# Both sample groups of an attention head turned, summed and closed together, the second cached values in the places of the cached keys, and fourteen heads' outputs kept whole

## The chip, the core and the metric

The kernel runs on one core of a Trainium2 chip. The metric is the device time of one execution in microseconds (us): the median of three runs before the change is 2847.96 us (2842.49 to 2850.93). The engines are TensorE (PE: matmuls and transposes; PEld is its weight load), VectorE (DVE), ScalarE (ACT), GpSimd (POOL) and SyncE (SP), which here only issues transfers.

## The reference

One step of a streaming encoder with two layers: a recurrent one (RG-LRU), then one of stick-breaking attention with 16 heads of 128. There is one prompt of 512 frames and there are 8 samples of 16 new frames each, and each sample has 512 cached keys and values. Only attention is touched here:

```python
def sb_block(q, q_pos, k, v):
    z = jnp.einsum('bqhd,bshd->bhqs', q, k).astype(jnp.float32) * (HEAD_DIM ** -0.5)
    mask = jnp.arange(k.shape[1])[None, :] < q_pos[:, None]
    log_keep = jnp.where(mask, jax.nn.log_sigmoid(-z), 0.0)
    log_after = lax.cumsum(log_keep, axis=3, reverse=True) - log_keep
    attn = jnp.where(mask, jnp.exp(jax.nn.log_sigmoid(z) + log_after), 0.0)
    return jnp.einsum('bhqs,bshd->bqhd', attn, v.astype(jnp.float32)).astype(q.dtype)

def stick_breaking_mixer(hn, k_all, v_all, w_in, w_out):
    q, zg = jnp.split(hn @ w_in, 2, axis=-1)
    o = stick_breaking(q.reshape(B, T, N_HEADS, HEAD_DIM), k_all, v_all)
    return (o.reshape(B, T, D_ATT) * jax.nn.silu(zg)) @ w_out
```

## The kernel before, in words

All is computed for 640 columns: 512 of the prompt, 128 of the samples. Products of large matrices are done in three matmuls of split numbers (`mm3`, lines 112 to 114: high times high, high times low, low times high), each split being a copy on ScalarE and a subtraction on VectorE. The recurrent layer, its output and the shared keys and values fill the span up to about 1985 us; then come the attention heads and the output product.

`heads` (line 1885) goes through 16 heads. While head h does its attention, the query and gate of head h+1 are computed in nine steps `q` of the generator `query`; in the last head the steps go to the output product instead. They are most of TensorE's work. The order of the steps inside a head is written out by hand in the strings `ORDER` and `LAST`; a scheduler then places the instructions on each engine's queue in about that order, moving what is ready by its own costs, and each queue is executed in order. The steps:

- `P`: the prompt's scores (tiles z, lines 1715 to 1717) and their weights (`sticks`, line 1641: on ScalarE Abs, Exp, Ln and a last Exp in line 1662; on VectorE an add, a scan and a subtraction; on GpSimd the mask). `X`: the samples' scores against their new keys (zn).
- `S0`, `S1`: scores of four samples each against their cached keys (zc, line 1757), weights into es0 and es1. The keys lie in two tiles ck of 128x1024 fp32. `S0` asks for the second group's keys; the step `N` (`cached_keys`, line 1692) for the next head's first.
- `V0`, `V1`: the prompt's weights turned on TensorE (pa, line 1727) and split into ath and atl (lines 1738, 1739).
- `T0`, `T1`: a sample group's weights turned (pas, line 1781) and copied by ScalarE to at. `T0` asks for the first group's cached values (cv).
- `O`: the prompt's output (po, lines 112 to 114), then the loads of the second group's cached values into the places of atl and ath (cva, cvb, line 1773), and of its new values on GpSimd's queue (line 1767).
- `M0`, `M1`: a sample group's output: 16 small matmuls against cached values (pos, line 1790) and 4 against new ones (line 1793), copied to ob. `C0`, `C1`: that output turned back (pot, line 1799), times the gate (line 1804).
- `L`, `K`: the next head's keys loaded (kr) and split (kh, kl, lines 1326, 1328). `U`, `W`: its values, loaded into the rest of cvb's place, and split. The gate's silu is made inside the query steps (ez, lines 1468 to 1473).

At the end of `C1` of heads 3, 5, 7, 9, 11 and 13 (`WHOLE`) the output is stored as it is, in fp32, and split when the output product loads it (`load` in `out_product`, lines 968, 969). Heads 0, 1, 2, 4, 6, 8, 10 and 12 split it at once (lines 1818, 1819) and store both halves (line 1821). Head 14 stays split in SBUF, head 15 whole.

PSUM has eight banks: two named halves, a ring of two (`one`) and a ring of four (`quad`).

Of the kernel before, what the change touches and what calls it, by code (L numbers as in the profile page):

```python
# [12 lines left out]
F32 = mybir.dt.float32  # L13
# [38 lines left out]
class Trunk:  # L52
# [1280 lines left out]
    def query_sums(self, ap):  # L1333
# [3 lines left out]
        flat = lambda tag: ap.tile([P, 3, 512], F32R, tag=tag, name="sum", bufs=1).rearrange("p a n -> p (a n)").bitcast(F32)  # L1337
# [179 lines left out]
    def query(self, h, ap):  # L1517
# [36 lines left out]
        def rest(a, c, u2, p5):  # L1554

            w = wl.pop(0), wl.pop(0)
            plain(c, w, 0)
            evac(halves[0], c, u2, ALU.add)
            self.scaled_query(0, halves[0], qh, ql, qs)
            yield  # L1560
            plain(a, w, 1)
            evac(halves[1], a, p5, ALU.add)
            self.scaled_query(1, halves[1], qh, ql, qs)
            with self.tc.issue_after(self.scaled):
                fill("wl", 3)
                fill("wh", 3)
            if h < NHEAD - 1:
                self.silu(ap, z, 0)
            yield
# [131 lines left out]
    def attention(self, h, ap, qkv, zs):  # L1701
# [17 lines left out]
        ath = ap.tile([P, 3, 512], F32R, tag="ath", name="ath", bufs=1)  # L1719
        atl = ap.tile([P, 3, 512], F32R, tag="atl", name="atl", bufs=1)  # L1720

        def spread(e, *rows, new=False):
# [5 lines left out]
            put = new_turn(0, ps) if new else lambda: None  # L1728
            parts, c = [], 0
            for i in rows:  # L1730
                m, q = min(i + 1, 3), slice(P * i, P * i + P)
                parts.append((ps[:, c : c + P * m].rearrange(pd, d=P), ath[:, :m, q], atl[:, :m, q]))
                if i == 3:
                    parts.append((ps[:, 384:], ath[:, 1, 0:P], atl[:, 1, 0:P]))
                c += P * (i + 1)
# [6 lines left out]
        def new_turn(g, ps):  # L1742

            tr(ps[0:TS, 384:], st[f"es{g}"][:, PAST : PAST + TS], self.ident)
            an = st["an"] = ap.tile([TS, P], F32, tag="an", name="an", bufs=1)

            def put():
                with self.tc.high_priority(200):
                    V.tensor_copy(an, ps[0:TS, 384:])

            return put

        def sample_scores(g):
# [10 lines left out]
        def new_values(g, t):  # L1764
            dma = (nc.gpsimd if g else nc.sync).dma_start
            rows = O["v"][TP + 64 * g : TP + 64 * g + 64, P * h : P * h + P]
            dma(t, rows.rearrange("(b t) d -> t b d", t=TS))
            return t
# [7 lines left out]
        def sample_turn(g):  # L1776
            e = st[f"es{g}"]
            st["cv"] = st["early"] if g else [cached_values(2 * u) for u in range(2)]
            ps = one("pas")
            for i in range(4):  # L1780
                tr(ps[:, P * i : P * i + P], e[:, P * i : P * i + P], self.ident)
            at = st["at"] = ap.tile([P, 4, P], F32, tag="at", name="at", bufs=1)
            A.activation(at, ps.rearrange(pd, d=P), AF.Copy)

        def sample_out(g):
            at, cvs = st["at"], st["cv"]
            po, an = one("pos"), st["an"]
            for i in range(4):
                for j in range(4):
                    mm(po[32 * j : 32 * j + 32, 0:P], at[:, i, 32 * j : 32 * j + 32], cvs[j // 2][:, 4 * (j % 2) + i, :],  # L1790
                       start=i == 0, stop=False, **kw)
            for j in range(4):
                mm(po[32 * j : 32 * j + 32, 0:P], an[:, 32 * j : 32 * j + 32], st["vn"][g][:, j, :], start=False, stop=True, **kw)
            ob = st["ob"] = ap.tile([P, P], F32, tag="ob", name="ob", bufs=1)
            A.activation(ob, po[:, 0:P], AF.Copy)

        def sample_close(g):
            ps = one("pot")
            tr(ps[:, 0:P], st["ob"], self.ident)
            if g == 0:  # L1800
                new_turn(1, ps)()
            cs = slice(TP + 64 * g, TP + 64 * g + 64)
            tv = "p (j t) -> p j t"
            V.tensor_tensor(o[:, cs].rearrange(tv, t=TS), ps[:, 0:P].rearrange(tv, t=32)[:, :, 0:TS],
                            zs[:, cs].rearrange(tv, t=TS), ALU.mult)
            if g == 1 and h == NHEAD - 1:
                self.local[h] = o
            elif g == 1 and h in self.STAY:
# [5 lines left out]
            elif g == 1 and h in self.WHOLE:  # L1814
                nc.gpsimd.dma_start(self.od[0][P * h : P * h + P, :], o)
            elif g == 1:
# [36 lines left out]
        def prompt_out():  # L1853
            po = zt("po")
            for i in range(3, -1, -1):
                th, tl = (x[:, 1, 0:P] if i == 3 else x[:, i, P * i :] for x in (ath, atl))
# [12 lines left out]
        st = {"vn": [new_values(0, ap.tile([TS, 4, P], F32, tag="vn", name="vn", bufs=1))], "early": []}  # L1869
        steps = {"P": prompt_scores, "X": new_scores, "O": prompt_out}  # L1870
        for g in range(2):
            steps[f"V{g}"] = lambda g=g: prompt_turn(g)
            steps[f"T{g}"] = lambda g=g: sample_turn(g)
            steps[f"M{g}"] = lambda g=g: sample_out(g)
            steps[f"C{g}"] = lambda g=g: sample_close(g)
# [5 lines left out]
    WHOLE = (3, 5, 7, 9, 11, 13)  # L1881
    LAST = "P c1 X S0 q q q S1 V0 q q T0 V1 Z O M0 T1 q q C0 M1 q C1 q"
    ORDER = "P q q c1 X S0 q q S1 V0 q q T0 V1 L q O U M0 T1 N K q C0 M1 W q"

    def heads(self, count=NHEAD):
        with self.pool("att") as ap:
# [11 lines left out]
            before, self.spare = {}, None  # L1898
            for h in range(count):
# [6 lines left out]
                for step in (self.ORDER if more else self.LAST).split():  # L1906
# [7 lines left out]
                    elif step == "c1":  # L1914
# [150 lines left out]
```

## Time and profile before

| | |
|---|---|
| profiled execution | 2848.22 us, span 2846.5 us, mean granted clock 0.998 |
| three runs | 2842.49, 2847.96, 2850.93 us |
| end of the first query | about 1984 to 2012 us |
| head 0 | about 2012 to 2060 us |
| heads 1 to 14 | about 2060 to 2605 us |
| head 15, with the first steps of the output product | 2605 to 2641 us |
| the rest of the output product | 2641 to 2833 us |
| rows of y, stores | 2833 to 2846.5 us |

The profile is of one execution, with times from the start of its span. A group or a wait is named by line, engine and tiles (out<-in). "A <- B" in a list of waits means that A's engine was idle until B was done. A stretch's row has the busy time and the number of instructions of each engine, the granted clock of TensorE (1.00 is full), the DMA engines' busy share and GB/s. Rows of a timeline give start, length, engine, line and, at the end in brackets, the idle time before it with what ended it. Matmuls overlap, so that their start, not their length, tells how fast they follow each other.

### The profile page before, as it was taken

The page shows a single profiled execution, that of the slowest core. Times are in us where ns is not written, and L with a number is a line of the kernel's source. Part 1 is how long each engine was busy: PE and PEld are TensorE (multiplying, and loading weights), DVE is VectorE, ACT ScalarE, POOL GpSimd, SP SyncE. Part 2 cuts the span into 40 slices and gives each one's busy share as a digit, 9 for nine tenths or more (in the row PEclk, how much of TensorE's full clock was granted, in tenths as well). Part 3 has the DMA queues.
Part 4 walks back from the last instruction along what each step waited for, and adds up shares of the span by engine and source line. Part 5 has one row for each costly group of instructions (what it writes and reads, how often), then busy time and mean ns, then how long its engine had stood idle before and what let it go on. Part 6 is the DMA issues. An engine that isn't in the chain of part 4 may idle for free.

```text
span 2846.5 us, 48073 instructions
## 1 busy us (share of the span) xinstructions
PE 2778.0 (98%) x18340; PEld 2454.0 (86%) x18340; DVE 2032.9 (71%) x3344; ACT 1667.3 (59%) x2862; POOL 426.9 (15%) x726
## 2 busy tenths in 40 slices
PE   6999999999999999999999999999999999999998
PEld 4799999999999987777777899967888888887887
DVE  7678777777677766766966866667877777777335
ACT  5466556655566655665756555553666766666223
POOL 0022212222222211111120000122101011011000
PEclk9999999999999999999999999999999999999999
DMA  9966767667666665685686333585476565668636
GB/s 338 328 147 155 164 160 161 148 164 164 158 149 163 149 228 202 203 251 181 222 286 216 100 107 114 173 274 202 131 215 193 187 198 168 205 197 267 189 111 229
DMA packets 245447, 540.57 MB, mean 190 GB/s; under 512 B 23048, under 2 KB 106120, under 8 KB 244064
## 3 DMA queue, kind: packets, MB, share of 16 engines
q1 hardware_dynamic: 198448, 375.08, 41.0%
q0 software_dynamic: 46768, 162.41, 23.0%
q8 instruction: 144, 2.36, 0.3%
q14 instruction: 87, 0.71, 0.1%
HBM read 498.01 MB, written 39.40 MB: 189 GB/s over the span
## 4 chain that ended last, share of the span: by engine, by line
PE 81%; DMA 4%; DVE 3%; ACT 2%; issue 2%; POOL 0%; SPq 0%; DVEq 0%; POOLq 0%; ACTq 0%
PE acc L112 7%; PE acc L114 6%; PE acc L113 6%; PE pa L112 4%; PE pa L114 4%; PE pa L113 4%; PE psh L112 4%; PE psh L114 4%; PE psh L113 4%; PE pc L114 3%; PE pc L112 3%; PE pc L113 3%; PE acck L112 2%; DMA cvb<-cache_v_dram 2%; PE acck L113 2%; PE acck L114 2%
## 5 line engine op out<-in xcount | busy, mean ns | idle before, releaser
L112 PE MATMUL acc<-wh,yh 128*128 128x512 f32 x940 | 369.6, 394 | 0.4 <-ACT wh L97 0.3
L113 PE MATMUL acc<-wl,yh 128*128 128x512 f32 x940 | 366.9, 390 | 1.5 <-DVE wl L98 1.4
L114 PE MATMUL acc<-wh,yl 128*128 128x512 f32 x940 | 365.6, 390 | 2.0 <-DVE yl L969 2.0
L98 DVE TENSOR_TENSOR wl<-wr,wh 128x1024 fp32r<-128x1024 f32 x151 | 186.2, 1237 | 215.7 <-ACT wh L97 215.2
L97 ACT ACTIVATE wh<-wr 128x1024 fp32r<-128x1024 f32 x151 | 159.6, 1058 | 266.8 <-PE acc L114 219.5
L112 PEld LDWEIGHTS acc<-wh,yh 128*128 128x128 f32 x940 | 176.2, 188 | 53.6 <-issue 16.1
L114 PEld LDWEIGHTS acc<-wh,yl 128*128 128x128 f32 x940 | 176.3, 188 | 39.8 <-DVE yl L969 2.8
L113 PEld LDWEIGHTS acc<-wl,yh 128*128 128x128 f32 x940 | 176.5, 188 | 39.3 <-DVE wl L98 4.1
L202 DVE TENSOR_TENSOR wa<-wa 128x1024 bf16<-128x1024 f32 (+1 forms) x160 | 191.3, 1247 | 10.0 <-ACT wa L201 9.6
L114 PE MATMUL pa<-xs,wl 128*128 128x320 f32 x630 | 194.8, 309 | 0.5 <-DVE wl L98 0.5
L112 PE MATMUL pa<-xs,wh 128*128 128x320 f32 x630 | 194.7, 309 | 0.0
L113 PE MATMUL pa<-xs,wh 128*128 128x320 f32 x630 | 194.7, 309 | 0.0
L97 ACT ACTIVATE wh<-sum 128x896 fp32r<-128x896 f32 x102 | 96.9, 950 | 143.2 <-PE pa L113 46.8
L201 ACT ACTIVATE wa<-wa 128x1024 bf16<-128x1024 f32 x160 | 159.8, 1047 | 25.0 <-DVE wa L202 12.1
L553 POOL DMA_DIRECT2D sum<-w_in_a_dram x90 | 79.4, 886 | 491.8 <-DVE wl L98 209.8
L112 PE MATMUL psh<-nh,wl 128*128 128x320 f32 x480 | 150.8, 314 | 0.0
L114 PE MATMUL psh<-nh,wl 128*128 128x320 f32 x480 | 148.4, 309 | 0.0
L113 PE MATMUL psh<-nl,wl 128*128 128x320 f32 x480 | 148.2, 309 | 0.0
L97 ACT ACTIVATE wh<-rv 128x256 fp32r<-128x256 f32 (+1 forms) x108 | 51.8, 480 | 145.6 <-PE pa L113 95.2
L114 PE MATMUL pc<-xs,wl 128*128 128x320 f32 x420 | 129.8, 309 | 0.7 <-DVE wl L98 0.7
L112 PE MATMUL pc<-xs,wh 128*128 128x320 f32 x420 | 130.1, 310 | 0.0
L113 PE MATMUL pc<-xs,wh 128*128 128x320 f32 x420 | 129.7, 309 | 0.0
(504 smaller groups left out, 8606.6 us busy)
## 6 DMA issues: line engine op xcount, KB each, us to landing
wa<-w_ada_dram POOLq DMA_DIRECT2D x120, 512.0 KB, 5.1
wr<-w_out_a_dram SPq DMA_DIRECT2D x96, 512.0 KB, 4.5
sum<-w_in_a_dram POOLq DMA_DIRECT2D x90, 448.0 KB, 5.7
wa<-w_ada_dram SPq DMA_DIRECT2D x72, 512.0 KB, 6.6
wr<-w_in_b_dram SPq DMA_DIRECT2D x64, 512.0 KB, 5.4
ck<-cache_k_dram SPq DMA_DIRECT2D x64, 512.0 KB, 5.9
wr<-w_out_b_dram SPq DMA_DIRECT2D x55, 512.0 KB, 4.0
raw<-w_in_a_dram SPq DMA_DIRECT2D x60, 448.0 KB, 4.0
```

Source lines behind the costliest of these rows:

```text
L97: self.split_at = nc.scalar.activation(hi[:, :n], raw, AF.Copy).ins
L98: nc.vector.tensor_tensor(lo[:, :n], raw, hi[:, :n].bitcast(F32), ALU.subtract)
L112: mm(out, sh, mh, start=start, stop=False, **kw)
L113: mm(out, sh, ml, start=False, stop=False, **kw)
L114: return mm(out, sl, mh, start=False, stop=stop, **kw)
L201: nc.scalar.activation(parts[i], raw, AF.Copy)
L202: nc.vector.tensor_tensor(parts[2] if i else raw, raw, parts[i], ALU.subtract)
L553: self.nc.gpsimd.dma_start(self.big[tag], self.quarter(w, i), accum_op=ALU.add)
```

## The change

Both sample groups are turned in one step `T` (the second group's transposes in a bank of the other ring), and the turned weights are copied back over es0 and es1 instead of into at. One step `M` sums both: first group's cached values, both groups' new values, second group's cached values. One step `C` in the next head closes both with two transposes and one product on VectorE. The second cached values are asked for in `S1`, into the two places of ck which its scores have just read. New values of all eight samples come in one load on the SP queue, at the head's start.

The next head's values are loaded into ath's place as a whole tile. ath and atl are laid out as rows of 1280 instead of 3x512, with the fourth block at 896. The first silu half waits for the last exponential of the sample weights on ScalarE (`issue_after`). All of heads 0 to 13 are `WHOLE`: one store, and the split in the output product. Before the first head, its keys and first cached keys are asked for ahead of the first query, and the keys no longer wait for the query's last load.

```diff
@@ flat tiles of query_sums, query
-        flat = lambda tag: ap.tile([P, 3, 512], F32R, tag=tag, name="sum", bufs=1).rearrange("p a n -> p (a n)").bitcast(F32)
+        flat = lambda tag: ap.tile([P, 2 * T], F32R, tag=tag, name="sum", bufs=1).bitcast(F32)
...
             if h < NHEAD - 1:
-                self.silu(ap, z, 0)
+                with self.tc.issue_after(self.weighed):
+                    self.silu(ap, z, 0)
@@ keys_load, values_load
-        with self.tc.issue_after(self.last_load):
+        with self.tc.issue_after(self.last_load) if h else ExitStack():
...
-        tile, self.spare = self.spare, None
-        if tile is None:
-            tile = ap.tile([P, 3, 512], F32R, tag="ath", name="vr", bufs=1).bitcast(F32)
-        raw = tile[:, 0, :].rearrange("p (t d) -> p t d", d=P)
+        tile = ap.tile([P, 2 * T], F32R, tag="ath", name="vr", bufs=1).bitcast(F32)
+        raw = tile[:, :TP].rearrange("p (t d) -> p t d", d=P)
@@ new_turn: both groups in V1
+            for g in range(2):
+                tr(ps[0:TS, 256 + P * g : 384 + P * g], st[f"es{g}"][:, PAST : PAST + TS], self.ident)
+            an = st["an"] = ap.tile([TS, 2 * P], F32, tag="an", name="an", bufs=1)
@@ sample_scores
             if g == 0:
                 self.ck = self.cached_keys(h, 1, ap)
+            else:
+                places = [ap.tile([P, 2, PAST], F32, tag="ck", name="cva", bufs=2) for _ in range(2)]
+                st["early"] = [cached_values(NB // 2 + 2 * u, c.rearrange("p a (i d) -> p (a i) d", d=P)) for u, c in enumerate(places)]
@@ sample_turn, sample_out, sample_close
+        def sample_turn():
+            st["cv"] = [cached_values(2 * u) for u in range(2)] + st["early"]
+            for g, ring in enumerate((one, zt)):
+                e, ps = st[f"es{g}"], ring("pas")
+                for i in range(4):
+                    tr(ps[:, P * i : P * i + P], e[:, P * i : P * i + P], self.ident)
+                A.activation(e[:, :PAST], ps, AF.Copy)
...
+            cached(0)
+            for g in range(2):
                 for j in range(4):
+                    mm(po[32 * j : 32 * j + 32, P * g : P * g + P], an[:, P * g + 32 * j : P * g + 32 * j + 32], st["vn"][:, 4 * g + j, :],
+                       start=False, stop=g == 0, **kw)
+            cached(1)
+            ob = st["ob"] = ap.tile([P, 2 * P], F32, tag="ob", name="ob", bufs=1)
+            A.activation(ob, po[:, : 2 * P], AF.Copy)
...
+            for g in range(2):
+                tr(ps[:, P * g : P * g + P], st["ob"][:, P * g : P * g + P], self.ident)
+            V.tensor_tensor(o[:, TP:].rearrange(tv, t=TS), ps[:, : 2 * P].rearrange(tv, t=32)[:, :, 0:TS],
+                            zs[:, TP:].rearrange(tv, t=TS), ALU.mult)
@@ prompt_out
             V.tensor_tensor(o[:, :TP], po, zs[:, :TP], ALU.mult)
-            t = ap.tile([P, 3, 512], F32R, tag="atl", name="cva", bufs=1).bitcast(F32)
-            self.spare = ap.tile([P, 3, 512], F32R, tag="ath", name="cvb", bufs=1).bitcast(F32)
-            places = (t[:, 0:2, :], self.spare[:, 1:3, :])
-            st["early"] = [cached_values(NB // 2 + 2 * u, c.rearrange("p a (i d) -> p (a i) d", d=P)) for u, c in enumerate(places)]
-            st["vn"].append(new_values(1, t[0:TS, 2, :].rearrange("p (b d) -> p b d", d=P)))
@@ orders
-    WHOLE = (3, 5, 7, 9, 11, 13)
-    LAST = "P c1 X S0 q q q S1 V0 q q T0 V1 Z O M0 T1 q q C0 M1 q C1 q"
-    ORDER = "P q q c1 X S0 q q S1 V0 q q T0 V1 L q O U M0 T1 N K q C0 M1 W q"
+    WHOLE = tuple(range(14))
+    LAST = "P c X S0 q q q S1 q V0 q q T V1 Z q O M q C q"
+    ORDER = "P q q c X S0 q q S1 V0 q q q T V1 L q O U K M N W q"
@@ heads
             out = self.attention_begin()
+            keys = self.keys_load(0, ap)
+            self.ck = self.cached_keys(0, 0, ap)
             self.first_query(ap)
-            self.spare = None
-            keys, values = self.keys_load(0, ap), self.values_load(0, ap)
-            self.ck = self.cached_keys(0, 0, ap)
+            values = self.values_load(0, ap)
```

More of the change, by code (lines that the diff above doesn't have):

```diff
@@ L1717, in score, with turned, block @@
             mm(out, ql[:, q], kh[:, :n], start=False, stop=True, **kw)
-        ath = ap.tile([P, 3, 512], F32R, tag="ath", name="ath", bufs=1)
-        atl = ap.tile([P, 3, 512], F32R, tag="atl", name="atl", bufs=1)
+        ath = ap.tile([P, 2 * T], F32R, tag="ath", name="ath", bufs=1)
+        atl = ap.tile([P, 2 * T], F32R, tag="atl", name="atl", bufs=1)
+        def turned(x, i):
+            if i == 0:
+                return x[:, 0:P]
+            return x[:, P:].rearrange("p (m s) -> p m s", s=FIRST)[:, : min(i + 1, 3), P * (i - 1) : P * i]
+        def block(x, i):
+            return x[:, 896:1024] if i == 3 else x[:, TP * i : FIRST * i + TP]
         def spread(e, *rows, new=False):
@@ L1727, in spread @@
                 tr(ps[:, P * j : P * j + P], e[:, P * j : P * j + P], self.ident)
-            put = new_turn(0, ps) if new else lambda: None
+            put = new_turn(ps) if new else lambda: None
             parts, c = [], 0
             for i in rows:
-                m, q = min(i + 1, 3), slice(P * i, P * i + P)
-                parts.append((ps[:, c : c + P * m].rearrange(pd, d=P), ath[:, :m, q], atl[:, :m, q]))
+                m = min(i + 1, 3)
+                src = ps[:, c : c + P * m]
+                parts.append((src.rearrange(pd, d=P) if i else src, turned(ath, i), turned(atl, i)))
                 if i == 3:
-                    parts.append((ps[:, 384:], ath[:, 1, 0:P], atl[:, 1, 0:P]))
+                    parts.append((ps[:, 384:], block(ath, 3), block(atl, 3)))
                 c += P * (i + 1)
@@ L1774, in cached_values @@
             return c
[L1776 to L1786, printed above, removed]
-            po, an = one("pos"), st["an"]
-            for i in range(4):
-                for j in range(4):
[L1790 to L1795, printed above, removed]
@@ L1797, in sample_close, with sample_out, cached @@
-        def sample_close(g):
+        def sample_turn():
[5 more added lines that the diff above has]
+                A.activation(e[:, :PAST], ps, AF.Copy)
+        def sample_out():
+            po, an = one("pos"), st["an"]
+            def cached(g):
+                e = st[f"es{g}"]
+                for i in range(4):
+                    for j in range(4):
+                        mm(po[32 * j : 32 * j + 32, P * g : P * g + P], e[:, P * i + 32 * j : P * i + 32 * j + 32],
+                           st["cv"][2 * g + j // 2][:, 4 * (j % 2) + i, :], start=g + i == 0, stop=g == 1 and i == 3, **kw)
+            cached(0)
+            for g in range(2):
+                for j in range(4):
+                    mm(po[32 * j : 32 * j + 32, P * g : P * g + P], an[:, P * g + 32 * j : P * g + 32 * j + 32], st["vn"][:, 4 * g + j, :],
[3 more added lines that the diff above has]
+            A.activation(ob, po[:, : 2 * P], AF.Copy)
@@ L1798, in sample_close @@
+        def sample_close():
             ps = one("pot")
[L1799 to L1802, printed above, removed]
+            for g in range(2):
+                tr(ps[:, P * g : P * g + P], st["ob"][:, P * g : P * g + P], self.ident)
             tv = "p (j t) -> p j t"
[L1804 to L1805 removed]
@@ L1813, in sample_close @@
                 self.local[h] = oh, ol
-            elif g == 1 and h in self.WHOLE:
+            elif h in self.WHOLE:
                 nc.gpsimd.dma_start(self.od[0][P * h : P * h + P, :], o)
-            elif g == 1:
+            else:
                 oh = ap.tile([P, T], F32R, tag="oh", name="oh", bufs=1)
@@ L1855, in prompt_out @@
             for i in range(3, -1, -1):
-                th, tl = (x[:, 1, 0:P] if i == 3 else x[:, i, P * i :] for x in (ath, atl))
+                th, tl = block(ath, i), block(atl, i)
                 self.mm3(po[:, P * i :], vh[:, i, :], vl[:, i, :], th, tl, i == 3, i == 0, **kw)
             V.tensor_tensor(o[:, :TP], po, zs[:, :TP], ALU.mult)
-            t = ap.tile([P, 3, 512], F32R, tag="atl", name="cva", bufs=1).bitcast(F32)
-            self.spare = ap.tile([P, 3, 512], F32R, tag="ath", name="cvb", bufs=1).bitcast(F32)
-            places = (t[:, 0:2, :], self.spare[:, 1:3, :])
-            st["early"] = [cached_values(NB // 2 + 2 * u, c.rearrange("p a (i d) -> p (a i) d", d=P)) for u, c in enumerate(places)]
-            st["vn"].append(new_values(1, t[0:TS, 2, :].rearrange("p (b d) -> p b d", d=P)))
         o = zs
@@ L1913, in heads @@
                         steps[step]()
-                    elif step == "c1":
+                    elif step == "c":
                         before.get(step.upper(), lambda: None)()
```

26 lines of the change are left out of this document (10 added, 16 removed).

## The prediction, made before the changed kernel ran

> **What bounds the kernel now.** I read the page's busy line first, then the busy time by stretches of the attention stage, then the waits of TensorE in it, then one head in order of time on TensorE, ScalarE, VectorE and the SP queue.
>
> ```profile
> PE 2778.0 (98%) x18340; PEld 2454.0 (86%) x18340; DVE 2032.9 (71%) x3344; ACT 1667.3 (59%) x2862; POOL 426.9 (15%) x726
> ```
>
> TensorE (PE) is busy for 98% of the span, so only what leaves it idle, or what it executes less of, can move the time. The next rows are stretches: length, then busy time and count of PE, PEld, DVE, ACT and POOL, then granted clock, DMA share and GB/s. They are the end of the first query, head 0 (two rows), heads 1 to 14, the end of head 14, head 15, and the output product.
>
> ```profile
> 1984.00:2012.00 28.00, 26.18 (x179) 25.91 (x177) 27.08 (x49) 14.53 (x34) 7.79 (x15) 1.00 0.46 139
> 2012.00:2045.00 33.00, 31.18 (x248) 27.57 (x248) 29.65 (x60) 25.35 (x59) 3.66 (x8) 1.00 0.39 130
> 2045.00:2060.00 15.00, 13.24 (x127) 11.42 (x120) 12.83 (x22) 10.03 (x23) 1.79 (x3) 1.00 0.75 199
> 2060.00:2590.00 530.00, 522.22 (x4547) 468.39 (x4546) 405.60 (x772) 358.61 (x814) 51.56 (x130) 1.00 0.63 195
> 2590.00:2605.00 15.00, 12.82 (x161) 10.05 (x159) 7.61 (x14) 6.43 (x14) 0.87 (x2) 1.00 0.93 305
> 2605.00:2641.00 36.00, 33.56 (x222) 23.88 (x219) 27.44 (x46) 25.39 (x51) 5.01 (x7) 1.00 0.85 289
> 2641.00:2833.00 192.00, 192.00 (x848) 158.90 (x848) 77.48 (x87) 60.32 (x83) 7.10 (x12) 1.00 0.56 171
> ```
>
> In heads 1 to 14 PE is idle for 7.8 of 530 us; in the output product never. VectorE has 124 us of slack in those heads, but is 97% busy just before head 0. These are the waits of PE from 2012 to 2650 us (total, times, longest):
>
> ```profile
> PE pos L1790 <- DMA cvb<-cache_v_dram: 9.6, 9, 1.5
> PE z L1715 <- ACT kh L1326: 2.4, 1, 2.4
> ...
> PE pos L1790 <- ACT qs L1459: 1.0, 1, 1.0
> PE pos L1790 <- ACT qh L1457: 0.8, 1, 0.8
> ...
> PE pos L1790 <- DMA cva<-cache_v_dram: 0.6, 1, 0.6
> ```
>
> So one place, the second sample group's output (M1, line 1790, output tile pos), collects 12.0 us: 9.6 + 1.0 + 0.8 + 0.6. Its values (cva, cvb) go into the places of the prompt's weights (atl, ath) and can't be fetched before the prompt's output has read these. One of those waits had a consequence:
>
> ```profile
> 2360.00:2363.00 3.00, 0.85 (x8) 0.31 (x6) 2.27 (x6) 2.12 (x5) 0.00 (x0) 1.00 0.85 237
> 2363.00:2366.50 3.50, 3.48 (x39) 2.47 (x40) 1.74 (x4) 0.80 (x2) 0.00 (x0) 0.56 0.94 281
> ```
>
> PE was busy for 0.85 of 3 us, and in the next 3.5 us the granted clock was 0.56, which costs 3.5 x (1 - 0.56) = 1.5 us.
>
> What all this costs shows in the distance of one head's first sample scores (zc) to the next head's. First and last of heads 1 to 14, and two neighbours without a wait, in the chain that ended last:
>
> ```profile
> 2061.59 0.88 PE zc L1757 x8
> ...
> 2257.51 0.87 PE zc L1757 x8
> ...
> 2295.93 0.88 PE zc L1757 x8
> ...
> 2572.20 0.87 PE zc L1757 x8
> ```
>
> A head without a wait takes 2295.93 - 2257.51 = 38.42 us. The 13 distances together are 510.61; 13 x 38.42 is 499.5. Waits, the slow clock and the refilling of the pipeline behind each wait thus cost **11.1 us** over heads 1 to 13.
>
> **The change, part by part.** *Second values earlier.* Their loads now wait for the second sample scores (S1), whose cached keys lie in the same places, and are read by a joint output M. The head between the two undisturbed neighbours, on PE:
>
> ```profile
> 2265.54 1.07 PE L1757 MATMUL zc<-ck,qs 128*32 128x512 f32 x8
> ...
> 2270.98 0.60 PE L1781 MATMUL pas<-ident,e 128*128 128x128 f32 x4
> ...
> 2277.28 1.08 PE L1790 MATMUL pos<-cv,at 128*32 128x128 f32 x32
> ...
> 2279.06 0.39 PE L112 MATMUL psh<-nh,wl 128*128 128x320 f32 x1
> 2279.29 0.31 PE L113 MATMUL psh<-nl,wl 128*128 128x320 f32 x1
> 2279.43 0.31 PE L114 MATMUL psh<-nh,wl 128*128 128x320 f32 x1
> ...
> 2282.77 0.27 PE L1744 MATMUL pot<-ident,e 128*16 128x128 f32 x1
> 2282.97 0.41 PE L1790 MATMUL pos<-cva,at 128*32 128x128 f32 x4
> ...
> 2284.58 0.51 PE L1715 MATMUL z<-kh,qh 128*128 128x512 f32 x1
> ```
>
> And on the SP queue, with the landing times (min/median/max) of the loads of ck, then of cv:
>
> ```profile
> 2268.31 0.89 SPq L1697 DMA_DIRECT2D ck<-cache_k_dram  x2
> 2277.15 0.37 SPq L1773 DMA_DIRECT2D cva<-cache_v_dram  x1
> ...
> 2280.26 1.98 SPq L1773 DMA_DIRECT2D cv<-cache_v_dram  x2
> ```
>
> ```profile
> DMA to landing us min/median/max: 3.4/5.9/8.4
> ```
>
> ```profile
> DMA to landing us min/median/max: 5.5/7.3/9.2
> ```
>
> Today cva is issued at 2277.15 and needed at 2282.97, 5.8 us later. After the change it is issued where the ck pair now stands (2268.31, second one 0.45 later) and needed in the second half of M, some 1.6 us (what M1 takes, 2282.97 to 2284.58) behind 2277.28, at about 2278.9: 10.1 us later, against a longest landing of 9.2. The wait goes in all heads: 11.1 us in heads 1 to 13, and in heads 0, 14 and 15 the rest of the 12.0. Since PE is idle for 7.8 us in all of 2060 to 2590, that rest is 12.0 - 7.8 = 4.2.
>
> *What comes late next: the next head's first keys.* They take the same two places, so they can start only when M ends. Today's M1 ends at 2284.58 and the next zc stands at 2295.93: 11.35 us, filled by prompt scores and two query steps, and the new order keeps these. The ck pair needs at most 8.4 from its issue; if both cv loads go first (1.98 us of queue), 10.4. Behind the waiting ck on SP stand the cv pair and the query's weights, and PE waits for neither kind today. I take nothing.
>
> *The turn T of both groups in one step.* It stands one query step later than T0 did, and wants the second group's weights (es1) earlier than T1 did. That step is 24 matmuls, 2279.06 to 2282.66 = 3.6 us (the transpose ahead of 2282.77 taken off), so T starts at 2270.98 + 3.6 = 2274.6 and its second half at 2275.0. On ScalarE and VectorE the chain of es1 looks so:
>
> ```profile
> 2268.73 0.49 ACT L1468 ACTIVATE ez<-z 128x320 f32<-128x320 f32 x1
> ```
>
> ```profile
> 2271.98 0.49 DVE L1471 SCALAR_TENSOR_TENSOR ez<-z,ez 128x320 f32<-128x320 f32 x1
> ```
>
> ```profile
> 2273.55 0.40 DVE L1739 TENSOR_TENSOR atl<-pa,ath 128x256 fp32r<-128x256 f32 x1
> ```
>
> ```profile
> 2274.84 0.65 ACT L1662 ACTIVATE e<-e 128x528 f32<-128x528 f32 x1 [0.77 <-DVE e L1661]
> ```
>
> The last exponential ends at 2275.5, 0.5 us too late as it stands. But the gate's silu (ez), which sits in between on both engines, now has to queue behind it, and the late split of atl moves behind T: some 0.4 us each, 1.2 together. I get es1 at 2274.3, 0.7 ahead. I take nothing; the bound is 0.5 a head, or 0.9 with one more operation in the way.
>
> *Joint steps.* The number of matmuls and transposes is the same; only changes of kind go. Behind today's T1 the first query matmul takes 2279.29 - 2279.06 = 0.23 instead of 0.14 (2279.43 - 2279.29), and from transpose to output matmul 0.20 pass (2282.77 to 2282.97) instead of the 0.11 between transposes, (0.60 - 0.27) / 3 by the pas and pot rows: 0.18 a head, 2.7 over 15. I take half, 1.3, since the scheduler may place other matmuls there; bounds 0 and 2.7. Fewer copies on ScalarE and VectorE are hidden under PE.
>
> *Fourteen outputs as fp32.* Eight heads lose one copy and one subtraction of 128x640 and one store; these lay under PE in heads with 124 us of VectorE slack: nothing. The output product gets eight more pairs of
>
> ```profile
> L968 ACT ACTIVATE yh<-yl x38: 717/723/764, 1016.4 to 2624.8; 128x640 fp32r<-128x640 f32 x38
> ```
>
> ```profile
> L969 DVE TENSOR_TENSOR yl<-yl,yh x38: 757/818/826, 1017.2 to 2627.1; 128x640 fp32r<-128x640 f32 x38
> ```
>
> that is 8 x 0.82 = 6.5 us on VectorE and 5.8 on ScalarE, and eight loads of 320 KB less. From 2590 to 2641 VectorE is idle for 7.4 + 8.6 = 16 us, which covers it if it can be used; beyond 2641 PE is always busy. On the other side the SP queue no longer stops for cva while weights stand behind it. Net 0. Bounds: -1.8 (the 36 - 33.56 = 2.4 that PE is idle in head 15, less the 0.6 counted above) and +5.7 (seven of the eight pairs, all on the path).
>
> *Keys of head 0 asked for before the first query.* The wait of 2.4 for kh can go, but VectorE is busy for 27.08 of the 28 us before it and holds up what follows: 0.5, bounds 0 and 2.4.
>
> **Sum:** 11.1 + 4.2 + 1.3 + 0.5 = 17.1. The profiled execution took 2848.2 us (span 2846.5 and 1.7 around it), the median of the three runs is 2848.0, so no correction: 2848.2 - 17.1 = **2831 us**. About 0.3%, 8.5 us, is what a measurement of this kernel can tell from no change.
>
> The clock: the row shows 0.56 right after 3 us with gaps of PE. The Trainium skill (TensorE: Matmul & The Clock Gate, Part 1: The HAM clock gate) says that the clock halves only after an idle window of about 3.4 us; by that these short waits were not the cause, and the dip would stay. It speaks against 1.5 us of my 11.1; the rows of this trace speak for them.
>
> **Rivals.**
> - *T waits for es1.* For it: 0.5 us are missing as the trace stands. Against: silu and atl leave the way. At 0.9 us in 14 heads 12.6 come back: 2843.6, no measurable change.
> - *Keys behind M are late: slower.* After M four loads of 512 KB (128 x 1024 fp32) and the prompt's values (256 KB) want to move, 2.36 MB. At the stage's mean of 195 GB/s these take 12.1 us, with 1.98 of queue ahead 14.1; then S0 waits 14.1 - 11.35 = 2.7 us in 14 heads, 38 us: 2869. It decides from 13.2 us on (1.83 a head, over 14 heads, eat 17.1 and 8.5 more). Against: the burst at the end of head 14 moved at 305 GB/s, so 7.7 us, and the longest landing of ck is 8.4.
> - *VectorE in head 15.* It is busy for 27.44 of 36 us there; if seven splits go on the path, 2831 + 5.7 = 2836.7, still faster.
> - *The dip is not due to the waits* (a clock gap that the change doesn't touch): 2831 + 1.5 = 2832.5.
>
> **How the numbers follow.** Chances: forecast 0.52, dip stays 0.08, head 15 0.10, T's wait 0.15, late keys 0.10, something unseen 0.05 (0.03 of it no change, 0.02 slower). Faster by over 0.3% (below 2839.4): 0.52 + 0.08 + 0.08 of head 15 = 0.68. Within: 0.02 + 0.15 + 0.03 = 0.20. Slower: 0.10 + 0.02 = 0.12. The range: below, all bounds at their best, 11.1 + 4.2 + 2.7 + 2.4 + 1.8 = 22.2, so 2826, and 3 for the spread of the runs (2842.49 to 2850.93 before): 2823. Above, T's wait with a little of head 15's: 2845. Late keys are left out.
>
> **What would show it.** Right: no wait of pos for cached values; zc to zc near 38.2 in every head; granted clock 1.00 from 2060 to 2590; eight more L968-L969 pairs without idle PE beside them. Wrong: PE waiting in the transposes of pas for the exponential (T), or in zc for ck (late keys), or PE idle grown beyond 2.4 us in head 15. The forecast falls if a head without waits takes longer than 38.4.

## The result and the profile after

The changed kernel is slower: 2862.09 us in the median of six runs (2857.2 to 2868.84) beside 2847.59 of the kernel before (six runs, 2842.49 to 2853.51), ratio 1.0052 with a 95% interval of 1.0034 to 1.0070. The forecast was 2831. The profiled execution took 2860.97 us, with a span of 2859.2. One run of experiment 3 (3113.47 us at a granted clock of 0.831, beside 0.994 to 0.996 in its other three) is left out of that experiment's numbers below, though the expectation of experiment 5 still counts it in.

The page's busy line, to be read beside that of before:

```profile
PE 2782.5 (97%) x18340; PEld 2456.7 (86%) x18340; DVE 2029.6 (71%) x3312; ACT 1662.2 (58%) x2846; POOL 415.5 (15%) x702
```

TensorE issues as many instructions as before (18340). It is 76.7 us idle in the span (2859.2 - 2782.5) instead of 68.5. The stretches say where: heads 2 to 14, head 15, and the output product (columns as in the prediction).

```profile
2100.00:2600.00 500.00, 484.82 (x4176) 430.89 (x4176) 366.14 (x679) 320.39 (x729) 37.65 (x102) 1.00 0.62 184
...
2618.00:2652.00 34.00, 30.68 (x199) 22.55 (x203) 29.84 (x48) 25.82 (x50) 7.16 (x6) 1.00 0.77 245
2652.00:2845.50 193.50, 193.50 (x882) 160.19 (x872) 76.38 (x86) 60.92 (x84) 7.05 (x12) 1.00 0.56 167
```

In heads 2 to 14 TensorE is idle for 15.2 of 500 us, where it was idle for 7.8 of 530. The waits of TensorE from 2005 to 2700 us name the new place:

```profile
PE zc L1768 <- DMA ck<-cache_k_dram: 16.3, 24, 2.0
PE pa L1755 <- POOL e L1667: 2.2, 1, 2.2
PE psh L112 <- DVE z L1546: 1.9, 1, 1.9
```

The 12.0 us of waits for cached values (pos, L1790) are gone, as forecast. In their place the sample scores (zc) wait for cached keys. The chain that ended last gives the distance of one head's first sample scores from the next head's; first and last of heads 1 to 14, and one head between:

```profile
2063.37 0.88 PE zc L1768 x8
...
2263.70 0.87 PE zc L1768 x8
...
2303.35 0.88 PE zc L1768 x8
...
2586.56 0.87 PE zc L1768 x8
```

The 13 distances together are 523.19 us, 12.58 more than the 510.61 of before. Head 1 starts 2063.37 - 2061.59 = 1.78 later, and what follows head 14's first scores is (2846.5 - 2572.20) - (2859.2 - 2586.56) = 1.66 shorter: 12.58 + 1.78 - 1.66 = 12.7, the difference of the two spans. So the question is what heads 1 to 13 lose.

**Which keys are late.** In the head that begins at 2263.5, SP's queue in the kernel before (at 2258, first scores at 2257.34) and, in the second fence, in the changed one:

```profile
2258.41 0.88 SPq L1697 DMA_DIRECT2D ck<-cache_k_dram  x2
2259.42 7.52 SPq L1366 DMA_DIRECT2D wr<-w_in_b_dram  x3
```

```profile
2265.91 0.34 SPq L1366 DMA_DIRECT2D wr<-w_in_b_dram  x1
2266.38 0.92 SPq L1696 DMA_DIRECT2D ck<-cache_k_dram  x2
2268.81 4.51 SPq L1366 DMA_DIRECT2D wr<-w_in_b_dram  x2
```

The second sample group's keys are asked for as soon as S0 has read the first group's, and S1 needs them 8.2 us after S0's start. Before, they were the first of the queue, 1.07 us after S0's start. Now, from head 2 on, one load of the next query's weights (wr, 512 KB) stands ahead of them, and it waits for a split on VectorE:

```profile
2265.20 0.69 DVE L1379 TENSOR_TENSOR wh<-wr,wh 128x512 fp32r<-128x512 f32 x1 [0.81 <-ACT wh L1378]
```

The split ends at 2265.89, the weight load is issued at 2265.91, the keys follow at 2266.38, 2.85 us after S0's start at 2263.53. No line of the diff orders this. In the program the weight load stands behind the keys (the edit of experiment 1 binds only loads traced after them, and it is enough), so it is the scheduler that moved it ahead when the steps around it changed. Why it did so isn't shown; experiment 4 rules out one cause.

**What one such wait costs.** TensorE at S1 in that head, from the last matmul of the query step (psh) to the first transpose behind the scores (pa):

```profile
2271.49 0.31 PE L114 MATMUL psh<-nh,wl 128*128 128x320 f32 x1
2272.26 1.05 PE L1768 MATMUL zc<-ck,qs 128*32 128x512 f32 x4 [0.46 <-DMA ck<-cache_k_dram]
2273.53 1.05 PE L1768 MATMUL zc<-ck,qs 128*32 128x512 f32 x4 [0.22 <-DMA ck<-cache_k_dram]
2274.51 0.33 PE L1736 MATMUL pa<-ident,e 128*128 128x128 f32 x1
```

The idle time shown is 0.46 + 0.22 = 0.68 us. But from start to start, 2271.49 to 2274.51, it takes 3.02, and the same piece without a wait takes 1.24 (experiment 1, rows there). The wait thus costs 1.78, and 1.10 of it no view counts as idle. The rows show where it goes. The eight matmuls of zc, four on each of the two tiles of keys, take 1.00 together when both tiles are there (experiment 1, 2272.67 to 2273.67); the four on the second tile take 0.98 alone here (2273.53 to 2274.51). So the matmuls of the two tiles run beside each other when they can, and when the second tile lands later than the first, its four come behind the others and cost nearly a whole round more. In every head from 2 to 13 but head 10, where a slow clock comes in between, the loss from start to start is 1.10 or 1.11 us more than the idle time shown, whether 0.37 or 2.28 us of idle time are shown.

### The profile page after: what moved, and what is told of

Read it like the earlier page. It is cut to its first block, busy times and chain, and to the rows that moved or that the text cites. A ratio compares the mean times of both kernels' runs of the same rounds, so it can differ in the third digit from the quotient of the medians.

```text
span 2859.2 us, 47887 instructions
## 1 busy us (share of the span) xinstructions
PE 2782.5 (97%) x18340; PEld 2456.7 (86%) x18340; DVE 2029.6 (71%) x3312; ACT 1662.2 (58%) x2846; POOL 415.5 (15%) x702
## 4 chain that ended last, share of the span: by engine, by line
PE 83%; DMA 4%; DVE 3%; issue 2%; ACT 1%; POOL 0%; SPq 0%; DVEq 0%; POOLq 0%; ACTq 0%
PE acc L112 7%; PE acc L114 7%; PE acc L113 7%; PE pa L112 4%; PE pa L114 4%; PE pa L113 4%; PE psh L112 4%; PE psh L114 3%; PE psh L113 3%; DMA ck<-cache_k_dram 3%; PE pc L114 3%; PE pc L112 3%; PE pc L113 3%; PE acck L112 3%; PE acck L113 3%; PE acck L114 2%
## 5 line engine op out<-in xcount | busy, mean ns | idle before, releaser
L112 PEld LDWEIGHTS acc<-wh,yh 128*128 128x128 f32 x940 | 176.4, 188 | 52.7 <-issue 15.2
L112 PE MATMUL pc<-xs,wh 128*128 128x320 f32 x420 | 130.1, 310 | 0.0
L98 DVE TENSOR_TENSOR wl<-sum,wh 128x896 fp32r<-128x896 f32 x102 | 110.9, 1087 | 26.7 <-ACT wh L97 26.6
```

The lines of the kernel that those rows point to most:

```text
L98: nc.vector.tensor_tensor(lo[:, :n], raw, hi[:, :n].bitcast(F32), ALU.subtract)
L112: mm(out, sh, mh, start=start, stop=False, **kw)
```

## Experiments

**1. The keys ahead of the weights.** In the changed kernel the weight loads of the query are traced so that they can't pass the second group's keys (keys_at is the second of the two loads):

```diff
     def query_load(self, h, i):
-            self.last_load = self.nc.sync.dma_start(self.qraw[i], ...).ins
+            with self.tc.issue_after(self.keys_at) if self.keys_at else ExitStack():
+                self.last_load = self.nc.sync.dma_start(self.qraw[i], ...).ins
     def cached_keys(self, h, g, ap):
+        if g == 1:
+            self.keys_at = last
```

> The changed kernel with one thing more: each weight load of the query that comes after the second cached keys in the program is queued behind them on SP, so that these keys (asked for when S0 has read the first) are no longer behind a weight load that waits for VectorE. Theory A, head of the line: the keys go out about 0.9 us after S0's start instead of 2.85, the waits of zc for ck (16.3 us in all) go but for a few tenths, and heads 2 to 13 fall from about 40.2 to 38.4 us each: 2862 - 12 x 1.7 - 2 for the slow clock behind one of them = 2840. Rival B, traffic: the keys land later because the values of both groups are now fetched together; then their landing stays at 6.5 us and more, S1 still waits 0.8 us a head, and the time is 2852 or more.

Measured: 2830.68 us (five runs, 2827.55 to 2843.12), ratio to the kernel before 0.9936 (0.9918 to 0.9955). The same place on TensorE:

```profile
2272.43 0.31 PE L114 MATMUL psh<-nh,wl 128*128 128x320 f32 x1
2272.67 1.07 PE L1771 MATMUL zc<-ck,qs 128*32 128x512 f32 x8
2273.67 1.09 PE L1739 MATMUL pa<-ident,e 128*128 128x128 f32 x8
```

and the first and last of the heads 1 to 14 in the chain, with the stretch between them:

```profile
2073.73 0.88 PE zc L1771 x8
...
2567.78 0.94 PE zc L1771 x8
```

```profile
2073.00:2567.00 494.00, 493.13 (x4395) 450.13 (x4395) 391.54 (x722) 339.19 (x769) 38.67 (x105) 1.00 0.64 193
```

(This profiled execution took 2843.12, the longest of the five, and is already 10.4 us behind the changed kernel's at head 1, in a part that the edit doesn't touch; only distances from there on are used.) The 13 distances are 494.05, so 29.14 less than in the changed kernel. Ten of the thirteen take 37.86 to 37.88, and no wait of zc for ck is left in them, so rival B falls. The 29.14 is the price of the keys' place, and it can be accounted for: from 2070 to 2600 the waits of the changed kernel show

```profile
PE zc L1768 <- DMA ck<-cache_k_dram: 15.2, 23, 2.0
```

which makes 15.2 + 12 x 1.10 = 28.4 with the hidden part of twelve heads, and one of the waits was followed by a slow clock:

```profile
2432.00:2434.00 2.00, 0.75 (x4) 0.17 (x4) 1.11 (x2) 0.30 (x1) 0.00 (x0) 1.00 1.00 352
2434.00:2437.50 3.50, 3.48 (x12) 1.36 (x11) 0.00 (x0) 0.02 (x1) 0.11 (x1) 0.51 0.76 243
```

3.5 x (1 - 0.51) = 1.7, together 30.1. (Experiment 1 isn't quite undisturbed itself: its heads 1, 3 and 9 take 38.89, 38.41 and 38.05.) The expectation let the heads fall to 38.4, the undisturbed head of the kernel before. They fell to 37.87, and so it came out too high, at 2840.

**2. The reverse.** In the kernel before, one weight load is put ahead of the second group's keys in heads 1 to 13:

```diff
@@ query_load
+        self.keys_now()
+
+    def keys_now(self):
+        load, self.keys_due = self.keys_due, None
+        if load:
+            with self.tc.issue_after(self.last_load):
+                self.ck = load()
@@ sample_scores
-                self.ck = self.cached_keys(h, 1, ap)
+                self.keys_due = lambda: self.cached_keys(h, 1, ap)
+                if not 0 < h < NHEAD - 2:
+                    self.keys_now()
```

> The kernel of before with the one change of order alone: in heads 1 to 13 a weight load of the query stands ahead of the second cached keys on SP, and the rest of the weight loads behind them, as in the changed kernel. Theory A: the keys go out about 1.4 us later than in the kernel before (its first weight load goes at 1.9 us after S0's start, the keys at 2.3 instead of 0.9), S1 waits 0.7 to 1.2 us in each of 13 heads: 2848 + 9 to 16 = 2857 to 2864. Rival B: the order costs nothing where the values' loads stand as before: 2848.

Measured: 2883.45 us (2877.69 to 2889.12), ratio 1.0126 (1.0104 to 1.0147). The waits from 2070 to 2600:

```profile
PE zc L1768 <- DMA ck<-cache_k_dram: 17.5, 22, 1.9
PE pos L1803 <- DMA cvb<-cache_v_dram: 4.9, 4, 1.5
```

With the hidden 1.10 in 13 heads the late keys cost 17.5 + 14.3 = 31.8 us, while the waits for values shrink from 8.7 to 4.9 in this stretch. The place alone, without the rest of the change, makes the old kernel slower too; the expectation was too low, above all by the hidden part. (5.6 of the 34.8 us between the two spans lie before head 1, so the median's 36 isn't all from here.)

**3. Six outputs stored whole, as before.**

```diff
-    WHOLE = tuple(range(14))
+    WHOLE = (3, 5, 7, 9, 11, 13)
```

> The changed kernel with only the six heads of before stored whole and the other eight split in the heads. Theory: the eight pairs of splits in head 15 hold up VectorE there, and GpSimd's mask beside it; then head 15 loses 2 to 4 us less: 2858 to 2860, and PE is idle for 1 us instead of 3.3 between S1 and the output of head 15. Rival: the splits lie under other work and the wait in head 15 has another cause: 2862, since the heads' own splits were hidden in the kernel before as well.

Measured: 2872.99 us (median of three runs, 2869.17 to 2876.97), ratio 1.0089 (1.0067 to 1.0111). This was a miss: storing fourteen whole helps the changed kernel by 2872.99 - 2862.09 = 10.9 us, and with six the waits of zc for ck grow from 16.3 to 19.5 us. A head that is split stores two halves of 320 KB instead of one, and they leave just when the keys are asked for. Rows of the chain behind the whole-stored head 11 and the split head 12:

```profile
2516.14 0.88 PE zc L1768 x8
...
2555.61 0.88 PE zc L1768 x8
...
2598.46 0.87 PE zc L1768 x8
```

39.47 us behind the whole output, 42.85 behind the split one (there with about half the clock for 3.5 us after its wait). Over all, heads 1 to 13 take 41.5 us on average behind the eight split outputs and 39.8 behind the five whole ones.

**4. The silu of the gate not held behind the exponential.**

```diff
             if h < NHEAD - 1:
-                with self.tc.issue_after(self.weighed):
-                    self.silu(ap, z, 0)
+                self.silu(ap, z, 0)
```

> The changed kernel without the edge that queues the first half of the gate's silu behind the last exponential of the second sample weights. Theory A: the keys' wait stays as it is, since the SP queue keeps its order; the silu's pieces go back between those of es1 and make T wait by 0.3 us or so in each of 14 heads: 2862 to 2867. Rival C: it is this edge that made the weight split late on ScalarE and with it the load ahead of the keys; then the wait of zc for ck falls below 8 us: 2853 or less.

Measured: 2868.69 us (2867.97 to 2876.2), ratio 1.008 (1.006 to 1.0099). T then waits for the weights, the keys' waits stay:

```profile
PE zc L1767 <- DMA ck<-cache_k_dram: 15.6, 25, 1.6
PE pas L1793 <- ACT e L1662: 7.7, 14, 1.6
```

7.7 us in 14 heads, 0.55 each: T needs the silu out of its way, and with it out of the way it hardly waits. The 6.6 us between the medians (2868.69 - 2862.09) fit that wait. Rival C falls: the keys' waits are 15.6 us, so this edge isn't what put the load ahead of the keys.

**5. Six stored whole, with the keys ahead** (the edits of 1 and 3).

> The kernel with the second group's keys ahead of the weights on SP, but with six outputs stored whole, as before the change; the other eight are split in their heads again. Theory A: storing whole helped by 12.9 us in the changed kernel (2874.98 against 2862.09) only because the split heads' two stores share the DMA engines with the late keys; with the keys asked for early nothing waits for them, PE covers the splits, and the time stays within 4 us of 2830.7, with no wait of zc for ck in heads 2 to 13. Rival B: the splits cost VectorE time on the path in every such head (8 x 1.6 us), wherever the keys stand: 2841 to 2845, and a distance of zc near 39.5 behind the split heads. Rival D: the six-whole version is faster, since the eight loads and splits more in head 15 fall away: 2825 to 2828.

Measured: 2837.58 us (eight runs, 2834.37 to 2844.86), ratio 0.9968 (0.9956 to 0.9981). The truth lies between the theories. No zc waits for ck in heads 2 to 13, and their distances are 37.9 to 38.8; but of the 10.9 us of experiment 3, 6.9 remain (2837.58 - 2830.68), and the intervals are too wide to tell these two differences apart. The profiles part them better. From head 1's to head 14's first scores six whole outputs cost 531.4 - 523.2 = 8.2 us more beside late keys (experiment 3 against the changed kernel) and 496.8 - 494.1 = 2.7 beside early ones (this run against experiment 1), so some 5.5 us come only with the late keys. From head 14's first scores to the end this run is 2.2 us behind experiment 1. A part of what remains shows in head 15, which has eight more halves to load:

```profile
PE pas L1797 <- DVE atl L1752: 2.1, 1, 2.1
PE acc L112 <- ACT wh L97: 1.9, 1, 1.9
```

```profile
2605.50:2616.00 10.50, 7.78 (x30) 5.28 (x30) 8.56 (x15) 7.78 (x17) 0.46 (x1) 0.67 1.08 364
```

PE is idle for 2.7 us of this stretch and the clock costs about 10.5 x (1 - 0.67) = 3.5 more, beside a wait of 2.2 us and 1.7 us of slow clock at the like place in experiment 1.

**6. Head 0's keys asked for after the first query, as before** (beside the edit of 1).

```diff
-            keys = self.keys_load(0, ap)
-            self.ck = self.cached_keys(0, 0, ap)
             self.first_query(ap)
-            values = self.values_load(0, ap)
+            keys, values = self.keys_load(0, ap), self.values_load(0, ap)
+            self.ck = self.cached_keys(0, 0, ap)
```

> The kernel with the second group's keys ahead of the weights on SP, but the keys and the cached keys of head 0 asked for after the first query, as before the change. The distance from head 0's to head 1's first sample scores was 46.1 us before, 47.5 in the changed kernel and 47.6 with the keys ahead. Theory A: the early loads delay the first query's last weights on SP and cost 1.5 to 2 us: 2828.5 to 2829.5, the distance back at 45.5 to 46, the wait of psh for z (1.9 us) gone and the wait for kh back. Rival: the 1.5 us belong to the joint output M in head 0, which stops for the prompt's split, so that the time stays at 2830 to 2832 and the distance at 47.6.

Measured: 2833.31 us (2830.17 to 2834.11), ratio 0.9947 (0.9933 to 0.9961); against 0.9936 (0.9918 to 0.9955) that is no difference that the runs can tell. The wait of psh for z falls from 1.9 us to 0.3 and the wait for kh comes back:

```profile
PE z L1717 <- ACT kh L1326: 2.1, 1, 2.1
```

One wait takes the other's place. The distance that the expectation went by misled: the wait for kh lies ahead of head 0's first scores, outside it.

**7. Head 15's small masks on VectorE** (beside the edit of 1). In the run of experiment 1 GpSimd took 3.07 us for a mask of 128 x 16 (at 2621.93), and TensorE waited 2.2 us for it:

```diff
             v = e[:, b - m.shape[1] : b]
-            nc.gpsimd.tensor_tensor(v, v, m, ALU.mult)
+            if self.masked:
+                nc.gpsimd.tensor_tensor(v, v, m, ALU.mult)
+            else:
+                with self.tc.high_priority(200):
+                    V.tensor_tensor(v, v, m, ALU.mult)
@@ heads
                 if not more:
                     self.behind = self.turned
+                    self.masked = False
```

> The kernel with the second group's keys ahead of the weights on SP, and in head 15 alone the two 128 x 16 masks of the sample weights on VectorE instead of GpSimd. There the mask of the second group took 3.07 us on GpSimd while VectorE was busy without a break, PE waited 2.2 us for it, and the clock then fell to 0.65 for 3.5 us. Theory: the wait goes but for VectorE's place in line, and the clock stays up: 1.5 to 3.5 us faster, 2827 to 2829. Rival: VectorE's queue in head 15 is the limit, the mask stands behind the splits of the stored outputs, and the wait moves to the next step: 2830 to 2832.

Measured: 2830.28 us (2827.7 to 2833.91), ratio 0.9938 (0.9925 to 0.9951). The wait of 2.2 us and the slow clock behind it are gone from the profile, and from head 14's first scores to the end it takes 268.9 us instead of the 273.8 of experiment 1. But the median is only 0.4 lower, which the runs can't tell from nothing. Nor is the gain in the profile shown to be the edit's: the profile of experiment 6, with all masks on GpSimd, has neither that wait nor the slow clock, and takes 270.3 us for the same part.

**8. The kernel before with fourteen outputs stored whole**, this part of the change alone.

> The kernel before with one part of the change alone: fourteen outputs stored whole instead of six. The prediction took this part at 0 (bounds 1.8 us faster and 5.7 slower). Theory A: eight stores fewer leave the late values (waits of pos for cva and cvb, 12.0 us in all) more of the DMA engines, so that 0 to 4 us are gained in heads 1 to 13, and head 15 pays 0 to 2 us: 2843 to 2848. Rival: the eight splits more lie on the path in head 15: 2850 to 2854.

Measured: 2846.77 us (twelve runs), ratio 0.9998 (0.9989 to 1.0008): no change.

**9. The second group's keys asked for on GpSimd's queue**, in the changed kernel, with SP's order kept.

```diff
-            self.nc.sync.dma_start(c, self.I["cache_k"][...])
+            (self.nc.gpsimd if g and h < NHEAD - 1 else self.nc.sync).dma_start(c, self.I["cache_k"][...])
```

> The changed kernel with one edit: the second group's cached keys of heads 0 to 14 are asked for by GpSimd's queue instead of SP's; everything on SP keeps its order, the weight load that stood ahead of the keys too. Theory A (it is the place in SP's queue, behind a weight load that waits for VectorE's split): the wait of zc for ck goes in heads 2 to 13 as it did with the keys moved ahead on SP, the distance of zc is 37.9, the time 2829 to 2834. Rival E (moving the keys ahead of the weights helped because the weights then came later and left the keys the DMA engines, not because of SP's queue): the weights still start first, so the keys still land late: 2845 to 2862, with a wait of zc for ck of 8 us or more in all.

Measured: 2884.24 us (2873.38 to 2886.67), ratio 1.0129 (1.0112 to 1.0146), worse than both theories. The keys gained nothing in time there: GpSimd's queue in one head (S0 starts at 2271.6), and SP's load of weights beside it:

```profile
2273.34 0.58 POOL L1832 DMA_DIRECT2D odl<-z  x1 [0.22 <-issue]
2273.94 1.43 POOL L1696 DMA_DIRECT2D ck<-cache_k_dram  x2
```

```profile
2273.83 7.39 SPq L1366 DMA_DIRECT2D wr<-w_in_b_dram  x3
```

They stand behind the last head's output store and are asked for 2.3 us after S0's start, while the weights are issued from 0.1 us earlier on. PE's waits of zc for ck add up to 28.9 us there (16.3 in the changed kernel). So the run didn't part SP's queue from the bytes ahead. The next one does.

**10. A sliver of the weights ahead of the keys, the rest behind.**

```diff
+            c = 32 if self.keys_at else 1024
+            self.last_load = self.nc.sync.dma_start(self.qraw[i][:, :c], ...).ins
+            if self.keys_at:
+                with self.tc.issue_after(self.keys_at):
+                    self.last_load = self.nc.sync.dma_start(self.qraw[i][:, c:], ...).ins
```

> The changed kernel, but every weight load after head 0's is cut in two: a sliver of 128 x 32 that keeps its place on SP (from head 2 on one stands ahead of the second group's keys and waits for VectorE's split as the whole load did), and the other 128 x 992 traced behind the keys. This parts two effects of the weight load ahead: SP's wait (the keys are asked for 2.85 us after head's first sample scores start instead of 0.9) and the 512 KB that move ahead of the keys (1.5 to 2 us at the stage's 250 to 330 GB/s). Theory A1 (SP's wait alone is enough): the keys are asked for as late as in the changed kernel, the wait of zc for ck stays at 8 us or more in all, and the time is 2848 to 2864. Theory A2 (the bytes ahead decide): the keys, asked for late but alone, land within the 8.2 us between the two sample scores, the wait all but goes, and the time is 2831 to 2840. Of an early ask alone 2831 is left.

Measured: 2831.6 us (six runs, 2828.76 to 2839.51), ratio 0.9941 (0.9925 to 0.9957). SP's queue in one head, and TensorE's two sample scores there:

```profile
2216.58 0.34 SPq L1367 DMA_DIRECT2D wr<-w_in_b_dram  x1
2217.05 0.92 SPq L1700 DMA_DIRECT2D ck<-cache_k_dram  x2
2218.31 0.34 SPq L1370 DMA_DIRECT2D wr<-w_in_b_dram  x1
```

```profile
2214.37 1.05 PE L1774 MATMUL zc<-ck,qs 128*32 128x512 f32 x8
2222.57 1.06 PE L1774 MATMUL zc<-ck,qs 128*32 128x512 f32 x8
```

The keys are asked for 2.68 us after S0's start, almost as late as in the changed kernel (2.85), and S1 starts 8.20 us after S0 without a wait. In heads 2 to 13 they are asked for 2.60 to 3.56 us after S0's start (2.61 to 2.93 in the changed kernel), and no view shows a wait of zc for ck. Measured from start to start, five of these heads still lose 0.1 to 1.1 us at S1, 2.8 in all, where the changed kernel loses 29.5. So the 512 KB that move ahead of the keys decide, and SP's wait for the split alone would have been covered. Theory A in the form that experiments 1, 2 and 9 were given, with SP's wait as the cause, falls; that the load ahead of the keys is the cause stands.

## Why the prediction was wrong

**The step that failed** is in the paragraph on what comes late next: "Behind the waiting ck on SP stand the cv pair and the query's weights, and PE waits for neither kind today. I take nothing." It looked at the first group's keys, behind M, and at what stands behind them. It never asked what would come to stand ahead of the second group's keys between S0 and S1, and took the order of SP's queue as fixed though the steps around it were rewritten. The price of that step was 29.1 us in heads 1 to 13: with it undone the time is 2830.7, beside the forecast of 2831. PE waiting in zc for ck was one of the prediction's own signs of being wrong; it came, but for the other group's keys.

**The rival that was slower** named the right resource, late cached keys, but put them in S0 behind M, where 11.35 us are left. Those keys came in time in heads 1 to 14; only head 15's S0 waited, 1.2 us. The wait was in S1, where 8.2 are left, and the traffic in its way was one weight load instead of the four loads and the prompt's values that the rival added up.

**The other terms, with the keys in their place** (experiment 1 against before; the medians differ by 2847.53 - 2830.68 = 16.9, forecast 17.1). That the sum comes out is in part luck. The interval of the ratio leaves 12.8 to 23.3 us, and the parts are off in both directions:

- *Heads 1 to 13:* 510.61 - 494.05 = 16.6, where 11.1 for the waits and some 0.09 a head for the joint steps were taken. An undisturbed head takes 37.87 us in experiment 1 instead of 38.42; the joint steps gave 0.55, three times the bound of 0.18. Most of it is in M. Before, M0 ran from 2277.28 until

```profile
2278.64 0.55 PE L1781 MATMUL pas<-ident,e 128*128 128x128 f32 x3
```

which is 1.36, and M1 took 1.61 (2282.97 to 2284.58), together 2.97. The joint M of experiment 1 takes 2291.06 - 2288.47 = 2.59:

```profile
2288.47 1.08 PE L1807 MATMUL pos<-cv,e 128*32 128x128 f32 x32
2289.48 0.64 PE L1813 MATMUL pos<-vn,an 16*32 16x128 f32 x16
2290.05 1.08 PE L1807 MATMUL pos<-cva,e 128*32 128x128 f32 x32
2291.06 0.51 PE L1717 MATMUL z<-kh,qh 128*128 128x512 f32 x1
```

so 0.38 of the 0.55; where the rest lies isn't shown. The head that the prediction took as undisturbed, since no wait was shown in it, was still losing 1.61 - 1.36 = 0.25 from start to start in M1, which has as many matmuls as M0.
- *Heads 0, 14, 15:* 4.2 and 0.5 were taken, and little of it came. From head 14's first scores to the end the profile of experiment 1 is 0.7 us shorter than that of before (2841.4 - 2567.78 = 273.6 beside 274.3), and head 0 to head 1 takes 1.5 longer. What went was replaced: in head 0 the wait for kh by one of 1.9 us for the gate's z and one of 1.1 for the prompt's split, in head 15 the old waits by 2.2 us for GpSimd's mask.
- *T's wait for es1:* nothing, as forecast, but for 0.6 us in one head of 1 to 14. Experiment 4 gives the price without the silu's move, 0.55 a head, where the prediction's bound was 0.5 and its slack was worked out from that very move.
- *Fourteen outputs as fp32:* net 0, and alone it is 0 (experiment 8). In company it isn't: 10.9 us to the good beside late keys (3 against the changed kernel), 6.9 beside early ones (5 against 1). The bound of 1.8 on that side was too narrow. It counted only PE's idle time in head 15; the longer waits for keys in experiment 3 show that the second stores also hold up other transfers. Where all of the 6.9 us lie isn't shown.
- *The clock:* the prediction took the dip of 1.5 us to be the waits' doing, against the Trainium skill (TensorE: Matmul & The Clock Gate, Part 1: The HAM clock gate), which has the clock halve after an idle window of about 3.4 us. In the changed kernel the clock fell to 0.51 behind one idle gap of 2.0 us, the longest wait of zc. The 1.00 that the prediction named as a sign (2060 to 2590) can't decide, since the row of before already reads 1.00 with the dip in it; shorter windows can. In the profiles of experiments 1, 5, 6, 7 and 10, where the keys come in time, heads 1 to 13 have no dip; before, in the changed kernel and in experiments 2, 3, 4 and 9 they have one to three. So the rows speak for the waits. But a wait isn't enough by itself: the 2.2 us for GpSimd's mask brought a dip in experiment 1 and none in the changed kernel, and experiment 8, with its waits for cached values, has none in heads 1 to 13. From 2000 us on every dip in these profiles lasts 3.5 us or some 7, at half the clock, and costs 1.7 us or twice that. What the gate counts as idle isn't shown.

## What to carry to other kernels

When a change rewrites the steps around a load, don't take the order of the queue from the old trace: list the new order and, for each load that has a deadline, the bytes that now move ahead of it, not only the time at which it is issued. A wait's idle time in a view is a lower bound: measure from start to start, against the same piece without a wait (here 1.78 us for 0.68 shown), and do the same for pieces that seem undisturbed. Where two tiles of an operand land one behind the other, look whether their matmuls could have run side by side. An effect that is nil alone, such as one store fewer in each head, can be worth several microseconds in company.

## What the runs showed of the hardware

A GpSimd multiplication of 128 x 16 that takes 0.21 us in the middle of the heads took 3.06 in head 15 of the changed kernel, while VectorE worked without a break on operations with two tensor inputs:

```profile
2640.76 3.06 POOL L1667 TENSOR_TENSOR e<-e,mask 128x16 f32<-128x16 f32 x1 [7.95 <-ACT e L1663]
```

```profile
2639.93 1.21 DVE L98 TENSOR_TENSOR wl<-wr,wh 128x1024 fp32r<-128x1024 f32 x1
2641.06 1.55 DVE L969 TENSOR_TENSOR yl<-yl,yh 128x640 fp32r<-128x640 f32 x2
2642.53 1.21 DVE L98 TENSOR_TENSOR wl<-wr,wh 128x1024 fp32r<-128x1024 f32 x1
```

It ended when VectorE paused, at 2643.8. The Trainium skill (GPSIMD Engine Reference, 1. Specifications) says that GpSimd shares its interfaces to the on-chip buffer with VectorE and contends with VectorE's instructions of two such inputs; the trace agrees, with 3.06 us for 0.21. The size varies: beside operations of that kind, head 15's second mask took 5.23 us in experiment 8, 1.19 in the kernel before and 0.37 in experiment 6, where it ended at 2613.5 while VectorE worked on:

```profile
2613.17 0.37 POOL L1668 TENSOR_TENSOR e<-e,mask 128x16 f32<-128x16 f32 x1 [8.24 <-ACT e L1664]
```

What lets it through sooner or later isn't shown.
